# One step of a streaming encoder on one core: three weight blocks begun on 704 tokens, between the adaLN sums

## The chip, the cores and the metric

The kernel runs on one core of one Trainium2 chip. The time is that of the device for one execution, in microseconds (us). Five engines work side by side, each through its own list of instructions in order, and wait for each other by semaphores: TensorE (PE in the profile; PEld is its loading of weights), VectorE (DVE), ScalarE (ACT), GpSimd (POOL) and SyncE (SP), which issues most of the transfers between HBM and SBUF. Results of matmuls land in PSUM, from which ACT or DVE copies them.

## What is computed

One trunk layer on 1024 prompt tokens and 32 sample tokens, each of these two streams with its own conditioning vector c. All arithmetic is in float32. Cut to what the change touches:

```python
mod = silu(c) @ w_ada + b_ada                 # w_ada: 1024 x 6144
sh1, sc1, gt1, sh2, sc2, gt2 = split(mod, 6)
h = rmsnorm(x, g_mix) * (1 + sc1) + sh1       # x: 1056 tokens x 1024 features
u = h @ w_in                                  # 1024 x 5640
qa, ka, va, qm, km, vm, om, ip, fp, ga, gm = split(u)
ya = band_attention(qa, ka, va, rel_bias)     # 8 heads x 64
ym = mlstm(...)                               # 4 heads x 128
merged = sigmoid(ga) * (ya @ w_br_att) + sigmoid(gm) * (ym @ w_br_mlstm)
x = x + gt1 * (merged @ w_out)
# then a second norm, a SwiGLU FFN with its own residual, and a last norm
```

## The kernel before

The activations stand with features on the 128 partitions and the 1056 tokens along the row, in three tiles of 352 tokens (`TILES`). The 1024 features are eight groups of 128, called features 0 to 7 below (`KD` = 8). A matmul in full float32 is made of three in a faster format: every operand is split into a high half (a rounded copy, made by ACT) and a low half (the rest, a subtraction on DVE or POOL), and `PASSES` multiplies high by high, low by high and high by low. So one weight block of 128 output columns costs 8 features x 3 passes = 24 matmuls ("products") of 128x352 for each token tile. `Weights` (W) holds the list of all blocks, loads their raw tiles ahead (three `wraw` buffers) and has them split ahead (four `wsp` half tiles). Buffers of 128 x 2112 floats are taken in turn from one pool of 16 (`slots`), rows of 1056 from a pool of four (`tmp`). The order on PE, ACT, DVE and POOL is the order in which the code is written (`manual_schedule`); SP's transfers are ordered by the framework's scheduler.

The head of the program, with which the change deals, runs so. x is loaded by tokens, eight tiles of 128 tokens and the sample's 32. PE transposes them to features (L281, L295), ACT copies the results to `xTs`, and DVE sums the squares of every token (L273). POOL takes the root of mean square + eps (L298, L299), and `bcast_cols` (L234) lays the 1056 scale factors out as a row over all partitions, `RB`. Meanwhile w_ada's columns for sh1 and sc1 (the first 2048) are loaded as eight tiles `was` of 128 rows, row group by row group. A sum over all 1024 rows is needed for each column, so no column is finished before the last tile is in. The scale sc1 is made on PE (L322): for every tile eight matmuls with the silu of c (`csil`), into one PSUM tile. The shift sh1 is made on DVE (`shift_part`, L309): products of each tile with the silu, accumulated in two rows `acv`, whose sums over partitions PE then takes (`row_sums`, L345).

`first_ada` (L316) and the lines from L1499 on write this order out. Then `first_units` (L467) takes the first two weight blocks, the K and the V block of the first pair of heads, feature by feature: `scaled_x` (L370) multiplies x with the scale and `RB`, `high_h` (L378) adds the shift and rounds, `low_h` (L388) makes the low half, and as soon as one feature of h stands, all 18 products of the two blocks with it run. Their six sums stand in six PSUM banks. After the eighth feature the K and V blocks copy their results (`k_block`, `v_block`), and the Q block (`q_block`) runs as an ordinary block, tile by tile (`unit`, L436). With the next K block begins the attention of the first two heads, whose steps are put between products. Its bias tiles come from a copy of the bias rows in HBM (`rb_d`) by a shifted read, issued when the head begins (`rel_bias_tile`, L688). x by features is also written to HBM (`xres`, L1508) and read again for the residual, much later.

## Time and profile before

| | us |
|---|---|
| median of three runs | 1599.96 (1599.67 to 1600.25) |
| the profiled execution: time | 1597.75 |
| the profiled execution: span, first to last instruction | 1596.1 |
| PE busy | 1566.1 |
| DVE busy | 1126.4 |
| ACT busy | 790.5 |
| POOL busy | 420.0 |

The span is that of the profiled execution, and what lies around it belongs to its time as well. Busy time is counted per engine, and several run at once. A row of a timeline gives the start, the duration, the engine, the line and operation, and the tiles: the one written, an arrow, those read; "x16" merges 16 instructions of a kind, and in square brackets stands how long the engine was idle before and what ended that. A row of a group has, behind the bar, the busy time of all in us and the mean of one in ns. A float32 matmul that is not split by hand shows as two instructions, a transpose as one.

### The profile page before, as it was taken

How to read it: one execution, taken by the hardware profiler on the slowest of the kernel's cores; microseconds unless marked ns; L12 is line 12 of the kernel's file. 1: busy time of each engine (PE TensorE's matmuls, PEld its weight loads, DVE VectorE, ACT ScalarE, POOL GpSimd, SP SyncE). 2: the span in 40 equal slices, each digit the busy share in tenths (PEclk: the TensorE clock that was granted, in tenths of full speed). 3: DMA queues.
4: the chain of work that ended last, by engine and by line, in shares of the span. 5: the costliest groups of instructions: out<-in, count | busy, mean ns of one | idle time of the engine just before them, and what ended most of it. 6: DMA issues, size and time to landing. Idle time of an engine off the chain costs nothing.

```text
span 1596.1 us, 27244 instructions
## 1 busy us (share of the span) xinstructions
PE 1566.1 (98%) x10167; PEld 1546.2 (97%) x10167; DVE 1126.4 (71%) x2291; ACT 790.5 (50%) x1735; POOL 420.0 (26%) x433
## 2 busy tenths in 40 slices
PE   7999999999999999999999999999999999999997
PEld 6989999999999999999999999999999999999997
DVE  7766555556776845546654699899888886799755
ACT  3665463544555545444433655544544444545443
POOL 0343242433222411000012100565565650000000
PEclk9999999999999999999999999999999999999999
DMA  9823323343132332675443311213222227427444
GB/s 364 265 83 94 98 82 109 86 135 110 43 94 67 88 86 75 133 257 176 133 145 112 106 54 54 95 57 103 81 80 94 68 78 252 143 80 249 130 136 155
DMA packets 209569, 193.48 MB, mean 121 GB/s; under 512 B 11530, under 2 KB 179118, under 8 KB 208414
## 3 DMA queue, kind: packets, MB, share of 16 engines
q1 hardware_dynamic: 206894, 189.92, 38.5%
q8 instruction: 80, 1.31, 0.4%
q10 hardware_dynamic: 2512, 1.77, 0.4%
q14 instruction: 51, 0.42, 0.1%
q0 software_dynamic: 32, 0.06, 0.0%
HBM read 153.24 MB, written 41.63 MB: 122 GB/s over the span
## 4 chain that ended last, share of the span: by engine, by line
PE 91%; DVE 3%; ACT 2%; DMA 2%; issue 1%; SPq 0%; POOL 0%; ACTq 0%; DVEq 0%; POOLq 0%
PE mm L443 41%; PE psb L1811 18%; PE mm L1811 11%; PE psb L2193 3%; PE mm L878 3%; PE mm L2193 2%; PE psV L783 2%; PE psb L2057 2%; PE psS L725 2%; PE psT L752 1%; DMA s<-in_w_ada_dram 1%; PE mm L2057 1%; DMA t<-in_x_sample_dram 1%; PE psV L1112 1%; PE mm L475 1%
## 5 line engine op out<-in xcount | busy, mean ns | idle before, releaser
L443 PE MATMUL mm<-s,wsp 128*128 128x352 f32 x4104 | 687.0, 324 | 0.0
L443 PEld LDWEIGHTS mm<-s,wsp 128*128 128x128 f32 x4104 | 657.3, 188 | 1.8 <-issue 0.4
L410 DVE TENSOR_TENSOR wsp<-wraw,wsp 128x512 fp32r<-128x512 f32 (+1 forms) x280 | 235.6, 858 | 114.1 <-ACT wsp L409 103.1
L1811 PE MATMUL psb<-s,wsp 128*128 128x352 f32 x1611 | 271.7, 322 | 1.6 <-DVE wsp L410 0.9
L409 ACT ACTIVATE wsp<-wraw 128x512 fp32r<-128x512 f32 x336 | 199.5, 617 | 142.4 <-PE psb L1811 44.5
L1811 PEld LDWEIGHTS psb<-s,wsp 128*128 128x128 f32 x1611 | 260.5, 188 | 2.1 <-DVE wsp L410 1.1
L1811 PE MATMUL mm<-s,wsp 128*128 128x352 f32 x933 | 159.3, 322 | 0.0
L1811 PEld LDWEIGHTS mm<-s,wsp 128*128 128x128 f32 x933 | 151.2, 188 | 0.5 <-DVE wsp L410 0.5
L745 POOL TENSOR_SCALAR st<-st,mx 128x640 f32<-128x640 f32 (+5 forms) x72 | 53.1, 738 | 186.2 <-DVE mx L744 171.2
L1207 DVE CUSTOM_DVE_ANT_0 junk<-wa,t 128x512 bf16<-128x512 f32 x128 | 94.7, 740 | 3.1 <-DMA wa<-in_w_mod_dram 2.1
L410 POOL TENSOR_TENSOR wsp<-wraw,wsp 128x512 fp32r<-128x512 f32 x56 | 74.9, 1357 | 57.1 <-ACT wsp L409 55.6
L739 DVE CUSTOM_DVE_ANT_0 st<-psS,bias 128x640 f32<-128x640 f32 (+5 forms) x72 | 44.5, 618 | 57.1 <-PE psS L725 41.9
L740 ACT ACTIVATE st<-st,mx 128x640 f32<-128x640 f32 (+5 forms) x72 | 47.9, 666 | 63.4 <-DVE mx L739 62.3
L1758 POOL TENSOR_TENSOR t<-t,sl 128x352 f32<-128x352 f32 x19 | 18.4, 969 | 212.8 <-ACT sl L1756 212.8
L759 ACT ACTIVATE pT<-psT 128x640 fp32r<-128x640 f32 (+3 forms) x80 | 38.7, 493 | 62.6 <-PE psT L752 47.6
L2166 POOL TENSOR_TENSOR fst<-fst,mhalf 128x6 f32<-128x6 f32 x1 | 2.3, 2312 | 221.1 <-DVE fst L2165 221.1
L764 DVE TENSOR_TENSOR pT<-psT,pT 128x640 fp32r<-128x640 f32 (+3 forms) x80 | 44.0, 558 | 22.2 <-ACT pT L759 22.2
L1420 POOL TENSOR_TENSOR wraw<-wraw,raw 128x512 f32<-128x512 f32 x33 | 55.8, 1705 | 0.9
L878 PE MATMUL mm<-s,s 128*128 128x264 f32 (+3 forms) x432 | 54.5, 283 | 0.0
L2193 PE MATMUL psb<-s,wsp 128*128 128x352 f32 x330 | 54.2, 324 | 0.0
L2193 PEld LDWEIGHTS psb<-s,wsp 128*128 128x128 f32 x330 | 53.1, 188 | 0.1
L878 PEld LDWEIGHTS mm<-s,s 128*128 128x128 f32 (+1 forms) x432 | 52.0, 179 | 0.5
(368 smaller groups left out, 2471.6 us busy)
## 6 DMA issues: line engine op xcount, KB each, us to landing
wraw<-in_w_in_dram SPq DMA_DIRECT2D x38, 512.0 KB, 4.0
wraw<-in_w_gate_up_dram SPq DMA_DIRECT2D x33, 512.0 KB, 3.9
wa<-in_w_mod_dram SPq DMA_DIRECT2D x64, 256.0 KB, 2.8
wraw<-in_w_down_dram SPq DMA_DIRECT2D x32, 512.0 KB, 4.3
a_d<-t SPq DMA_DIRECT2D x22, 528.0 KB, 2.7
g_d<-t SPq DMA_DIRECT2D x16, 528.0 KB, 3.2
x<-xres SPq DMA_DIRECT2D x16, 528.0 KB, 7.1
t<-g_d SPq DMA_DIRECT2D x16, 528.0 KB, 4.5
```

Of the source, the lines that this page charges most:

```text
L409: act.activation(dst[:, 0], src, AF.Copy)
L410: eng.tensor_tensor(dst[:, 1], src, f(dst[:, 0]), op=ALU.subtract)
L443: pe.matmul(pt[:, :hi - lo], wt[(w0 + k) // 4][:, a, (w0 + k) % 4], xt[k][:, b, lo:hi], start=(k == 0 and q == 0), stop=(k == n - 1 and q ...
L739: dve.tensor_tensor_reduce(so, sv, bi, -1.0, 3.0e38, ALU.add, ALU.min, mx[:n, 1:2])
L740: act.activation(st[:n, :w], st[:n, :w], AF.Exp, bias=mx[:n, 1:2], scale=-1.0, accum_out=mx[:n, 2:3])
L745: pool.tensor_scalar(st[:n, :w], st[:n, :w], mx[:n, 3:4], 1.0, op0=ALU.mult, op1=ALU.mult)
L878: pe.matmul(pt[:n, :wd], hs[k][:, a, i * P:i * P + n], whl[b][:, k, :wd], start=(k == 0 and q == 0), stop=(k == KD - 1 and q == 2))
L1207: dve.tensor_tensor_reduce(junk, wa, crow[:, c], 1.0, 0.0, ALU.mult, ALU.add, at)
L1420: self.eng.tensor_tensor(a(dst), a(x), a(y), op=op)
L1811: pe.matmul(acc, wt[:, a, k], x[k][:, b], start=(start and not onto and k == 0 and q == 0), stop=(stop and k == 3 and q == 2), skip_group_ ...
L2057: pe.matmul(acc, wt[k // 4][:, u, k % 4], piece_of[k, i][:, v], start=(k == 0 and q == 0), stop=(k == KP - 1 and q == 2))
L2193: pe.matmul(acc, wt[(k - k0) // 4][:, u, (k - k0) % 4], piece_of[k, 2][:, v], start=(k == 0 and q == 0), stop=(k == NF - 1 and q == 2))
```

## The change

The tensors reach the kernel in other layouts. x comes by features (`x_t`: 8 x 128 x 1056, prompt and sample together), so that no transposes are needed. w_in comes by blocks of 128 columns, each partition's 1024 values of a block in one run of 4 KB. The first 2048 columns of w_ada come by feature: tile j has all 1024 rows for the 128 scale columns of feature j, and beside them the 128 shift columns of the same feature, for features 0 to 2 laid out like the scale's, for the others with the columns on partitions and the 1024 rows along the row. So one tile finishes one feature. The bias rows come shifted, 128 x 640 per head. Nothing is written to `xres` or `rb_d`; the residual is read from `x_t`.

The head is written anew:

- The first 704 tokens (two tiles, `CUT`) go ahead, the last 352 follow ("late"). SP loads the early part of x by features, the first adaLN tile in between, then half of the raw weights of three blocks (K, V and Q), the next adaLN tiles, the late part of x, and the rest.
- Squares are taken by ACT over whole feature rows, DVE adds them to one row `acc` (`square_sum`), PE sums that over partitions (`token_sums`), DVE and POOL make the factors (`token_roots`).
- `scale_sums(j)` is eight float32 matmuls for feature j's scale (with `i` = 1, its shift), placed between the products; `scale_done` and `shift_done` finish them on ACT. From feature 3 on the shift comes from `shift_sums`: a multiplication with reduction on DVE, over the row `crow` of the silu of c, once for each stream, finished by ACT.
- For every feature the 18 early products are three blocks x three passes x two tiles. The late tokens follow at the end with two blocks, K and V (48 products); the Q block makes its third tile as an ordinary unit.
- `late_h(k)` makes the late part of the features in three steps, each a feature behind the other: scaling, high half, low half. The sample's 32 columns go through POOL for scaling and low half.
- `put` copies the K block's first tile while the late products run. The loads of the cache and of the first two bias tiles are issued at round 5.

The core of the diff:

```diff
-            sp.dma_start(wa, w_ada[len(was) * P:(len(was) + 1) * P, 0:2048])
+        for i in range(2):
+            sp.dma_start(wa[:, i], w_ada[i, j])
...
+    def scale_sums(j, i=0):
+        at = P * (2 * i + j % 2)
+        for k in range(KD):
+            pe.matmul(psH[:, at:at + P].rearrange("p (r c) -> p r c", c=2), was[j][:, i, k * P:(k + 1) * P],
+                      csil[:, k].unsqueeze(1).to_broadcast([P, DH, 2]), start=(k == 0), stop=(k == KD - 1),
+                      skip_group_check=True)
+    def shift_sums(j, c):
+        dve.tensor_tensor_reduce(junk, was[j][:, 1], crow[:, c], 1.0, 0.0, ALU.mult, ALU.add, sha[:, c, j:j + 1])
+        act.activation(sh1[:, c, j:j + 1], sha[:, c, j:j + 1], AF.Identity, bias=cols[:, R_ADA + j:R_ADA + j + 1])
...
+        for k in range(1, KD):
+            products(k, 0)
+            if k + 2 < KD:
+                scale_sums(k + 2)
+                scale_done(k + 2)
...
+            low_h(k, 0, CUT)
+            if k + 1 < KD:
+                scaled_x(k + 1, 0, CUT)
+                high_h(k + 1, 0, CUT)
...
+            if k + 2 < KD:
+                shift_sums(k + 2, 0)
+            products(k, 1)
...
+            if 1 <= k <= 3:
+                first_high(k - 1, 1)
                 first_low(k - 1, 1)
+            if SHIFT_PE <= k + 1 < KD:
+                shift_sums(k + 1, 1)
+            if k >= 5:
+                late_h(k - 5)
+            products(k, 2)
+            if k == 5:
+                W.loaded = W.split_n = 3
+                W.load(6)
+                early_loads.append(cache_loads())
+                early_loads.extend(rel_bias_tile(h) for h in range(2))
+        for k in range(3, KD + 2):
+            late_h(k)
+            if k == 7:
+                put(*early[0], pts[0][0][:, :NT])
+        put(*early[1], pts[0][1][:, :NT])
+        for k in range(KD):
+            for q in range(3):
+                for i in range(2):
+                    product(k, i, q, 2)
```

Three places of the compiled order. On PE, ahead of the first products and behind them (L322 before and L328 after are the adaLN sums, with a tile `s` of w_ada; L475 the products, with a feature of h and a half tile of a weight): before, the last two of the eight adaLN steps, the row sums and the first products,

```order
L322 MATMUL psT_267<-csil,s_126 128x128 x8
L322 MATMUL psT_267<-csil,s_128 128x128 x8
L348 MATMUL psV_266<-ones,t_268 128x64 x2
L348 MATMUL psV_266<-ones,t_269 128x64 x2
L348 MATMUL psV_266<-ones,t_268 128x64 x2
L348 MATMUL psV_266<-ones,t_269 128x64
L352 MATMUL psV_266<-csil,s_128 128x64
L348 MATMUL psV_266<-ones,t_269 128x64
L352 MATMUL psV_266<-csil,s_128 128x64
L348 MATMUL psT_267<-ones,t_268 128x64
L475 MATMUL mm_426<-s_432,wsp_398 128x352
L475 MATMUL psS_425<-s_432,wsp_400 128x352
```

and now, from the end of the transposes that lay out the token factors:

```order
L227 MATMUL mm_254<-ident,roots 128x64
L475 MATMUL mm_264<-s_268,wsp_246 128x352
L475 MATMUL psS_155<-s_268,wsp_259 128x352
L475 MATMUL psT_153<-s_268,s_262 128x352
L475 MATMUL mm_265<-s_268,wsp_246 128x352
L475 MATMUL psS_155<-s_268,wsp_259 128x352
L475 MATMUL mm_266<-s_268,s_262 128x352
L328 MATMUL psV_154<-csil,s_118 128x128 x16
L475 MATMUL mm_264<-s_268,wsp_246 128x352
L475 MATMUL mm_265<-s_268,wsp_246 128x352
```

Two sums of one feature now stand behind the first six products, where all adaLN sums stood ahead of the first one.

On DVE, one feature's round (L375 and L350: scaling; L392 and L369: low half; L465 and L442: a weight's low half; L337: the shift's reduction and the read of its result). Before, features 2 and 3:

```order
L375 SCALAR_TENSOR_TENSOR s_486<-s_111,s_271,t_265 128x1024
L375 SCALAR_TENSOR_TENSOR s_486<-s_111,s_271,t_265 128x32
L392 SCALAR_TENSOR_TENSOR s_514<-s_486,sh_270,s_514 128x1024
L465 TENSOR_TENSOR wsp_401<-wraw_295,wsp_401 128x512
L375 SCALAR_TENSOR_TENSOR s_545<-s_112,s_271,t_265 128x1024
L375 SCALAR_TENSOR_TENSOR s_545<-s_112,s_271,t_265 128x32
L392 SCALAR_TENSOR_TENSOR s_541<-s_486,sh_270,s_541 128x1024
```

and now a round of one feature, with the beginning of the next:

```order
L369 SCALAR_TENSOR_TENSOR s_368<-s_96,sh_151,s_368 128x704
L350 SCALAR_TENSOR_TENSOR s_96<-s_96,s_152,t_146 128x704
L337 ISA t_147,sha<-s_131,s_102 128x1024
L337 ISA sha 128x1
L442 TENSOR_TENSOR wsp_260<-wraw_100,wsp_260 128x512
L337 ISA t_147,sha<-s_128,s_102 128x1024
L337 ISA sha 128x1
L369 SCALAR_TENSOR_TENSOR s_406<-s_96,sh_151,s_406 128x704
L350 SCALAR_TENSOR_TENSOR s_97<-s_97,s_152,t_146 128x704
```

Two reductions over 1024 elements, with their reads, have come into the round; the rows of 1024 became rows of 704.

On POOL, the sample's columns (L394 before: the low half alone; L352 after: scaling, L371: low half) and the split of a weight (L410). Before:

```order
L394 TENSOR_TENSOR s_541<-s_486,s_541 128x32
L394 TENSOR_TENSOR s_568<-s_545,s_568 128x32
L394 TENSOR_TENSOR s_594<-s_545,s_594 128x32
L394 TENSOR_TENSOR s_621<-s_598,s_621 128x32
L410 TENSOR_TENSOR s_631<-wraw_300,s_631 128x512 x2
L394 TENSOR_TENSOR s_658<-s_598,s_658 128x32
```

and now, all in the late part:

```order
L352 TENSOR_TENSOR s_97<-s_97,t_146 128x32
L371 TENSOR_TENSOR s_368<-s_96,s_368 128x32
L352 TENSOR_TENSOR s_97<-s_97,t_146 128x32
L371 TENSOR_TENSOR s_406<-s_96,s_406 128x32
L352 TENSOR_TENSOR s_98<-s_98,t_146 128x32
L371 TENSOR_TENSOR s_447<-s_97,s_447 128x32
L352 TENSOR_TENSOR s_98<-s_98,t_146 128x32
L371 TENSOR_TENSOR s_484<-s_97,s_484 128x32
L371 TENSOR_TENSOR s_519<-s_98,s_519 128x32
L371 TENSOR_TENSOR s_560<-s_98,s_560 128x32
```

POOL has two operations for each feature, the scaling two features ahead of the low half, where it had one.

More of the change, by code (lines that the diff above doesn't have):

```diff
@@ L334, in first_load @@
[L334 to L353 removed]
+    xTp = [slot([P, 2, T]) for _ in range(KD // 2)]
@@ new lines, in hybrid_stream_step, with in_block, load_ada, load_first @@
+    xTs = [xTp[j // 2][:, j % 2] for j in range(KD)]
+    CUT = TILES[2][0]
+    first_cols = (KA, VA, QA)
+    first_ws = [wraw.tile([P, KD, P], F32, tag="wraw", name=nm("wraw")) for _ in first_cols]
+    was = []
+    def in_block(c):
+        return w_in[(c - GA) // P + 28 if c >= GA else c // P]
+    def load_ada():
+        j = len(was)
+        wa = slot([P, 2, D])
+        for i in range(2):
+            sp.dma_start(wa[:, i], w_ada[i, j])
+        was.append(wa)
+    def load_first(half):
+        for raw, c in zip(first_ws, first_cols):
+            sp.dma_start(raw[:, 4 * half:4 * half + 4], in_block(c)[:, 4 * half:4 * half + 4])
@@ new lines, in silu_cols, with square_sum, token_sums @@
+    def silu_cols():
+        act.activation(csil, cols[:, R_C:R_C + 16].rearrange("p (c k) -> p k c", c=2), AF.Silu)
+        dve.scalar_tensor_tensor(gb1, cols[:, R_ADA + 8:R_ADA + 16], 1.0, gm1, op0=ALU.add, op1=ALU.mult)
+    def square_sum(j, lo, hi):
+        n = hi - lo
+        o = sq2[:, j % 2, :n] if j else acc[:, :n]
+        act.activation(o, xTs[j][:, lo:hi], AF.Square)
+        if j:
+            dve.tensor_tensor(acc[:, :n], acc[:, :n], o, op=ALU.add)
+    def token_sums(a0, n, at, r):
+        for i, a in enumerate(range(0, n, P)):
+            b = min(a + P, n)
+            pe.matmul(tok[:b - a, at + r * i:at + r * (i + 1)], acc[:, a:b], ones[:, 0:1].to_broadcast([P, r]),
+                      start=(i == 0), stop=True, skip_group_check=True)
@@ L473, in product, with products @@
         def product(k, i, q, t):
             (a, b), (lo, hi) = PASSES[q], TILES[t]
-            pe.matmul(pts[i][t][:, :hi - lo], wts[i][k // 4][:, a, k % 4], hs[k][:, b, lo:hi],
+            out = last[i] if t == 2 else pts[i][t]
+            pe.matmul(out[:, :hi - lo], W.blocks[i][3][k // 4][:, a, k % 4], hs[k][:, b, lo:hi],
                       start=(k == 0 and q == 0), stop=(k == KD - 1 and q == 2))
-        for t, (lo, hi) in enumerate(TILES):
+        def products(k, q):
+            for i in range(3):
+                for t in range(2):
+                    product(k, i, q, t)
@@ L521, in first_units @@
+        put(*early[1], pts[0][1][:, :NT])
[3 more added lines that the diff above has]
+                    product(k, i, q, 2)
+        first[id(W.blocks[0])] = {2: last[0][:, :NT]}
+        first[id(W.blocks[1])] = {0: pts[1][0][:, :NT], 1: pts[1][1][:, :NT], 2: last[1][:, :NT]}
+        first[id(W.blocks[2])] = {0: pts[2][0][:, :NT], 1: pts[2][1][:, :NT]}
+        for w, n in zip(W.blocks, (3, 3, 2)):
+            for _ in range(n):
                 W.used(w)
+        W.advance()
@@ L538, in w_cols @@
     def w_cols(c0, home=None):
-        return weight([w_in[:, c0:c0 + P]], KD, 3, home)
+        return weight([in_block(c0)], KD, 3, home)
     plan = []
@@ L1496, in hybrid_stream_step @@
         W.add(w)
-    first_ada()
-    first_split(0)
-    row_sums(0, 0, 2)
-    row_sums(1, 0, 2)
-    row_sums(0, 2, 4)
-    row_sums(1, 2, 4)
-    first_scale()
-    row_sums(0, 4, 5)
-    for j in range(KD):
-        sp.dma_start(xres[j], xTs[j])
-    first_units([run.w for run in segs[0][1][:2]])
+    first_units(segs[0][1][0].put)
     W.ahead = 2
```

401 lines of the change are left out of this document (196 added, 205 removed).

## The prediction

> **What bounds the kernel now.** I read the page first: the shares, the strip of forty slices and the chain of work that ended last.
>
> ```profile
> span 1596.1 us, 27244 instructions
> PE 1566.1 (98%) x10167; PEld 1546.2 (97%) x10167; DVE 1126.4 (71%) x2291; ACT 790.5 (50%) x1735; POOL 420.0 (26%) x433
> ...
> PE   7999999999999999999999999999999999999997
> ...
> PE 91%; DVE 3%; ACT 2%; DMA 2%; issue 1%; SPq 0%; POOL 0%; ACTq 0%; DVEq 0%; POOLq 0%
> ```
>
> TensorE (PE) is busy for 98% of the span and holds 91% of the chain. A change can only gain where PE waits, or by giving it less to do. The strip shows where it waits: the first slice and the last. So the table of stretches comes next (columns: PE, weight loads, DVE, ACT and POOL busy, granted clock, DMA share, GB/s).
>
> ```profile
> 10.00:20.00 10.00, 8.37 (x71) 7.21 (x70) 7.85 (x14) 8.06 (x22) 2.04 (x2) 1.00 1.03 397
> 30.00:40.00 10.00, 8.58 (x72) 8.01 (x72) 8.51 (x11) 1.26 (x2) 0.00 (x0) 1.00 1.06 336
> 40.00:50.00 10.00, 8.81 (x59) 8.25 (x59) 9.87 (x20) 6.59 (x15) 0.62 (x2) 1.00 0.77 281
> 80.00:100.00 20.00, 19.14 (x121) 18.50 (x120) 14.04 (x31) 14.13 (x32) 9.89 (x13) 1.00 0.39 123
> 100.00:120.00 20.00, 17.98 (x127) 17.31 (x127) 10.88 (x26) 13.64 (x24) 6.48 (x8) 1.00 0.15 41
> 200.00:1500.00 1300.00, 1294.96 (x8390) 1284.30 (x8388) 935.26 (x1917) 643.34 (x1419) 354.90 (x340) 1.00 0.36 110
> ```
>
> Up to 40 us PE is partly idle and the DMA engines are full (share 1.03 to 1.06), at 336 to 397 GB/s. From 40 to 50 us DVE is the full one. Stretches of 80 to 120 us hold 2.9 us of idle PE; the 1300 us that follow hold 5.0 in all. The head is the place, so I read PE's timeline there.
>
> ```profile
> 14.63 1.42 PE L281 MATMUL mm<-ident,s 128*128 128x128 f32 x11 [0.96 <-DMA s<-in_x_prompt_dram]
> ...
> 20.69 3.88 PE L322 MATMUL psT<-csil,s 128*128 128x128 f32 x32
> ...
> 35.86 2.05 PE L322 MATMUL psT<-csil,s 128*128 128x128 f32 x16 [0.54 <-DMA s<-in_w_ada_dram]
> ...
> 37.75 1.67 PE L348 MATMUL psV<-ones,t 128*128 128x64 f32 x14
> ...
> 40.97 0.43 PE L475 MATMUL mm<-s,wsp 128*128 128x352 f32 x1 [0.66 <-ACT s L386]
> ```
>
> The last of eight x tiles lands at 14.6, the last adaLN tile at 35.9, and the first product of a block with the features (L475) starts at 40.97. Everything ahead of it is bought by DMA: the products wait until all of x and all of w_ada's first 2048 columns are in.
>
> I need one place where the same work is done in both kernels. It is the end of the 216 products (9 tiles of 24) of the first K, V and Q blocks.
>
> ```profile
> 68.52 5.55 PE L443 MATMUL mm<-s,s 128*128 128x352 f32 x33
> 73.90 0.60 PE L612 MATMUL mm<-ident,t 128*128 128x128 f32 x4
> 74.26 2.17 PE L443 MATMUL mm<-s,s 128*128 128x352 f32 x12
> ...
> 81.25 6.05 PE L443 MATMUL mm<-s,wsp 128*128 128x352 f32 x36
> 87.14 0.34 PE L725 MATMUL psS<-s,s 128*128 128x128 f32 x2
> ```
>
> The Q block ends at 81.25. Two groups of four V transposes stand inside it, 73.90 to 74.26 and one like it, that the changed kernel has later: 0.7 us. So the place stands at **80.5** before. The last two rows give a product: 36 from 81.25 to 87.14, 0.163 each.
>
> **The change part by part.** *The start of the products.* Needed now are the early 704 tokens of x (8 x 0.360 MB) and one adaLN tile (1.05 MB): 3.93 MB, where the last x tile before was the end of 4.19 MB. At 0.397 MB/us (10 to 20 us) this is 0.7 us earlier than 14.63: 13.9. Behind that stands a chain; its prices:
>
> ```profile
> L1756 ACT ACTIVATE sl<-x 128x352 f32<-128x352 f32 x21 | 10.5, 498 | 38.8 <-DVE x L1750 36.5 <-DVE rs L1578 2.2
> L465 DVE TENSOR_TENSOR wsp<-wraw,wsp 128x512 fp32r<-128x512 f32 x4 | 2.6, 680 | 0.0
> L1138 POOL TENSOR_TENSOR dn<-dn,mhalf 128x2 f32<-128x2 f32 x16 | 12.1, 759 | 1.3
> L1588 POOL TENSOR_TENSOR rs<-rs,mhalf 128x4 f32<-128x4 f32 x3 | 3.2, 1081 | 19.5 <-DVE rs L1586 19.5
> L461 ACT ACTIVATE wsp<-wraw 128x512 fp32r<-128x512 f32 x4 | 2.4, 623 | 15.6 <-DMA wraw<-in_w_in_dram 15.6
> L375 DVE SCALAR_TENSOR_TENSOR s<-s,s,t 128x352 f32<-128x352 f32 x4 | 2.2, 578 | 0.1
> L386 ACT ACTIVATE s<-s,sh 128x352 fp32r<-128x352 f32 x4 | 2.2, 588 | 4.3 <-DVE s L375 2.3 <-DVE sh L360 2.1
> ```
>
> Square of 704 on ACT: about 0.8 (0.50 for 352, 0.3 of it growing with size); the addition on DVE 0.9 (0.68 for 512); six sums with ones, seven of them in 1.67 above: 1.4; two small scalings 0.3; the root of three columns on POOL, between 0.76 for two and 1.08 for four: 0.9; three transposes 0.4; copy of the row to SBUF 0.5. That makes 19.1 for the first row. The second root follows on POOL (0.9) and, with some 0.1 for each hand-over between engines, its row is copied at about 20.5. ACT then has two weight copies (0.57 each without overlap) ahead of the first high half, which takes 0.59: **22.2**, 18.8 us ahead of before. Bounds: 21.2 if ACT's copies pack closer, 24.2 if short rows slow the transfers to the 336 GB/s of 30 to 40 us.
>
> *What PE has to do from there to the common place.* 216 x 0.163 = 35.2. The adaLN sums that stood ahead of the products now stand among them: feature 0's two are ahead, features 1 and 2 bring two each, 3 to 7 one each: 9. One is eight matmuls; the row at 20.69 is two such blocks in 3.88, so 1.94: 17.5. Three late token sums and three late transposes: 1.0. In sum 53.7, where before had 35.2 and 11 of the row sums seen at 37.75 (0.24 each, 2.6). Without a wait the place would stand at 75.9.
>
> *Waits among them.* DVE now makes five features' shift rows by a reduction over 1024 elements for each of two streams, and the low halves and scaling for 704 tokens. A round is one feature's 18 early products.
>
> ```profile
> L375 DVE SCALAR_TENSOR_TENSOR s<-s,s,t 128x1024 f32<-128x1024 f32 x6 | 7.6, 1274 | 0.0
> L273 DVE CUSTOM_DVE_ANT_0 t<-s 128x1024 bf16<-128x1024 f32 x8 | 9.7, 1225 | 6.2 <-DMA s<-in_x_prompt_dram 6.0
> L386 ACT ACTIVATE s<-s,sh 128x1024 fp32r<-128x1024 f32 x6 | 6.9, 1153 | 4.4 <-DVE s L375 3.1 <-DVE sh L360 0.7 <-DMA xres<-s 0.6
> ```
>
> 704 lies between 0.578 and 1.274: 0.94, less 0.06 by which such instructions overlap: 0.88. A reduction and its read are 1.24. Rounds 2 and 3 have 2 x 0.88 + 2 x 1.24 + 0.62 for a weight's low half; that low half also waits 0.9 for ACT's copy, which stands on ACT behind the bias that needs the reduction just made. 5.8 on DVE against 18 x 0.163 + 1.94 = 4.9 on PE. Round 1 is even, 4 and 5 are under PE (4.2 and 4.8, the latter with the first late scaling), round 6 is over it by 0.6, as PE has no sum there (2.9). Excess 0.9 + 0.9 + 0.6; a little slack from round 0 goes off it. I take **2.2**; bounds 0.5 (all reductions overlap) and 4.0 (every 704 costs 1.1). ACT has about half of that per round (one high half of 704 at 0.9, a weight copy at 0.6 and small biases) and hides.
>
> *The late third.* 48 products, 0.98 per feature, already in the 216. Beside them DVE has 0.96 (a scaling and a low half of 320 tokens), ACT 1.1, POOL two operations on the sample's 32 columns:
>
> ```profile
> L394 POOL TENSOR_TENSOR s<-s,s 128x32 fp32r<-128x32 f32 x8 | 4.7, 592 | 38.2 <-ACT s L386 36.6 <-DMA xres<-s 1.7
> 64.58 1.24 POOL L394 TENSOR_TENSOR s<-s,s 128x32 fp32r<-128x32 f32 x1
> ```
>
> 2 x 0.59 = 1.18 per feature on POOL, over PE's 0.98; but POOL starts two features ahead, and 0.2 x 8 = 1.6 is covered by that lead. Zero taken, bounds 0 and 6 (the rival below).
>
> So the place stands at 22.2 + 53.7 + 2.2 = **78.1** against 80.5: **-2.4**.
>
> *Behind it.* Before, the Q block was a cushion of 12 us in which ACT and DVE caught up with K and V. Now it is one tile (3.9 us), and all three blocks' copies come at once: about 9 us on ACT (15 copies of 0.46 and three weight copies). The V transposes inside K block 1 wait for a PSUM buffer that ACT frees as the copies end, some 0.4 us. In return the first scores no longer stand behind the cache's low halves on DVE, since those come after them. What PE waited for there:
>
> ```profile
> L553 ACT ACTIVATE s<-mm 64x352 fp32r<-64x352 f32 x20 | 9.1, 456 | 8.8 <-PE mm L443 5.1 <-PE mm L475 3.6
> ...
> 90.30 0.50 PE L725 MATMUL psS<-s,s 128*128 128x256 f32 x2 [0.86 <-DVE mx L739]
> ...
> 103.14 0.63 PE L752 MATMUL psT<-ident,st 128*128 128x128 f32 x4 [0.29 <-DVE pT L764]
> ...
> 106.09 0.59 PE L783 MATMUL psV<-pT,s 128*128 128x256 f32 x3 [1.74 <-ACT pT L759]
> ```
>
> The first wait (0.86) is that queue on DVE; I halve it. The other two come when ACT loads tables for Exp, Silu and Exp again; ACT's rows there keep their order, so they stay. +0.4 - 0.4 = **0**; bounds -2.9 (all three go) and +1.5.
>
> *Nothing on the path:* w_in by block, the shifted bias rows, the copies of x and of the bias that are no longer written to HBM, loads moved in SP's queue. No PE wait of the page names w_in or the bias; full DMA engines hide or free them. If that cover fails, K block 1's raw weights come later: 14.3 MB of first loads and 2.7 MB of bias, cache and raw weights in front of and with them are in at 47 us by 0.4 MB/us, and they are needed at 74.
>
> *The clock.* PE's transposes of 128 x 128 in the first 5 us, and later:
>
> ```profile
> L281 PE MATMUL mm<-ident,s 128*128 128x128 f32 x16 | 3.9, 425 | 5.3 <-DMA s<-in_x_prompt_dram 5.3
> ...
> L281 PE MATMUL mm<-ident,s 128*128 128x128 f32 x49 | 6.5, 284 | 1.6 <-DMA s<-in_x_prompt_dram 1.3 <-ACT s L282 0.3
> ```
>
> 425 ns against 284: PE starts slow. And in the tail, after the last matmul (1586.9):
>
> ```profile
> 1586.62 0.27 PE L2116 MATMUL psb<-ident,x 128*96 128x128 f32 x1
> ...
> 1590.00:1592.00 2.00, 0.00 (x0) 0.00 (x0) 0.40 (x1) 0.76 (x2) 0.00 (x0) 0.50 1.02 378
> ```
>
> the granted clock falls to 0.50. So PE slows when it idles for two or three us, and needs until about 9 us to be fast. In the changed kernel PE has only 2.2 us of work from 14 to 22.2, with a last gap of 2.3 us, so the first products may run slow for some 4 us at a price between 0 and 2.0. I take 0.9. [...]
>
> **Sum:** -2.4 + 0 + 0.9 = -1.5. The profiled execution took 1597.75 us (span 1596.1 and 1.7 around it): 1596.2. The median of the runs is 1599.96, 2.2 above that execution, so **1598.5** there. About 0.2% (3.2 us) is what a measurement of this kernel can tell from no change.
>
> **The rivals.**
> 1. *All waits go.* DVE keeps up (-2.2), the clock stays (-0.9), and attention's waits fall by 1.5. For it: DVE's total from 22 to 66 us (15 operations on 704, 10 reductions, 6 low halves, 7 additions, 4 late ones: 34 us by the prices above) is under PE's 42. Against: its order. 1598.5 - 4.6 = 1593.9.
> 2. *POOL's sample columns become the bound; slower.* Each late feature's third pass waits for POOL's two operations in order. Mean 0.59 us, but the last of them above took 1.24, beside a busy DVE, and DVE is never idle there now. Behind round 7, from about 64.5 us, 13 of them remain, and PE could end the third at 74: from 0.7 us apiece the lead is spent, and at 1.24 they end 6.6 us late: 1605.1. Against: seven of eight before were under 0.9. [...]
> 3. *The early start does not come off.* x by feature has rows of 2816, 1408 and 2048 bytes in place of 4 and 8 KB; at 336 GB/s the start is 24.2 and the gain is spent: 1600.5.
>
> **How the numbers follow.** The forecast has 0.38, rival 3 0.07: no difference, 0.45. Rival 1 and mixtures beyond 3.2 us: 0.33 faster. Rival 2, and DVE's upper bound with the cold clock: 0.22 slower. The range reaches from rival 1 with attention's lower bound (1592.5) to rival 2 (1605). The forecast's own range is 1596 to 1602.
>
> **What would show it.** Right: first L475 product near 22; PE rounds of about 4.9 us with small waits on DVE's low halves and ACT's high halves; the 216 products done near 78; the scores' waits near 103 and 106 still there, some us earlier. Wrong: PE waiting for POOL in the late third; adaLN sums waiting for DMA (each should find its tile landed); matmuls at 0.3 us after 22; attention's first rounds without waits; or a changed stretch after 200 us, where I expect none.

## The result, and the profile after

| us | before | after |
|---|---|---|
| median, 8 runs of each | 1599.62 | 1605.09 (1601.66 to 1606.28) |
| ratio to before, 95% interval | | 1.0031 (1.0020 to 1.0043) |
| the profiled execution: time | 1597.75 | 1605.54 |
| its span | 1596.1 | 1603.5 |
| its mean granted clock | 0.998 | 0.993 |

The changed kernel is slower by about 5 us, where 1598.5 was forecast and 1605.0 was the end of the range. Three executions in the groups of runs of this document (3969 and 5767 us of the kernel before, 3117 us of e13_two) stand far apart, and the ratios leave them out. Of the changed kernel's page, the lines that answer to those shown of before:

```profile
span 1603.5 us, 27214 instructions
PE 1567.5 (98%) x10133; PEld 1547.0 (96%) x10133; DVE 1114.0 (69%) x2296; ACT 798.8 (50%) x1757; POOL 416.2 (26%) x439
...
PE   6989999999999999999999999999999999999997
...
PEclk8999999999999999999999999999999999999999
...
PE 89%; DVE 4%; ACT 4%; issue 1%; DMA 0%; POOL 0%; SPq 0%; ACTq 0%; DVEq 0%; POOLq 0%
```

PE's busy time is the same within 1.4 us and the span is 7.4 longer. The loads no longer stand in the chain (DMA 2% before). What is new is the strip of the granted clock, which starts with an 8. Before it was

```profile
PEclk9999999999999999999999999999999999999999
```

The table of stretches says where (columns as before: PE, weight loads, DVE, ACT, POOL, granted clock, DMA share, GB/s):

```profile
10.00:20.00 10.00, 4.96 (x42) 4.59 (x42) 3.85 (x7) 6.13 (x11) 1.20 (x2) 0.91 1.03 403
20.00:30.00 10.00, 7.96 (x40) 7.12 (x40) 3.84 (x6) 2.92 (x6) 0.49 (x1) 0.58 1.04 409
30.00:40.00 10.00, 9.29 (x76) 9.00 (x75) 6.35 (x10) 5.52 (x14) 0.00 (x0) 1.00 1.03 402
100.00:120.00 20.00, 17.57 (x107) 16.64 (x105) 9.55 (x26) 13.55 (x27) 6.19 (x7) 0.91 0.13 41
```

From 20 to 30 us the clock was at 0.58 (1.00 before), and PE "busy" for 7.96 us did 40 instructions, where it did 76 in 9.29 us right after. From 100 to 120 us it was at 0.91. PE's timeline of the changed kernel, with the places by which the two kernels can be laid beside each other:

```profile
19.72 1.81 PE L227 MATMUL mm<-ident,roots 128*128 128x128 f32 x6 [1.91 <-POOL roots L322]
23.57 0.66 PE L475 MATMUL mm<-s,wsp 128*128 128x352 f32 x1 [2.04 <-ACT s L360]
...
25.50 5.15 PE L328 MATMUL psV<-csil,s 128*128 128x128 f32 x32
...
37.82 2.05 PE L328 MATMUL psV<-csil,s 128*128 128x128 f32 x16 [0.71 <-ACT sh L342]
...
57.72 0.59 PE L475 MATMUL mm<-s,wsp 128*128 128x352 f32 x2 [0.26 <-ACT s L360]
...
66.46 0.59 PE L475 MATMUL mm<-s,wsp 128*128 128x352 f32 x2 [0.60 <-ACT s L360]
...
76.69 0.40 PE L475 MATMUL psT<-s,wsp 128*128 128x352 f32 x1 [0.66 <-POOL s L371]
...
81.90 1.60 PE L417 MATMUL mm<-s,wsp 128*128 128x352 f32 x9
...
95.89 0.62 PE L775 MATMUL psS<-s,s 128*128 128x384 f32 x2 [0.85 <-DVE mx L789]
...
99.82 0.41 PE L802 MATMUL psT<-ident,st 128*128 128x128 f32 x2 [1.38 <-DVE pT L814]
...
107.67 0.63 PE L802 MATMUL psT<-ident,st 128*128 128x128 f32 x4 [0.57 <-DVE pT L814]
...
110.62 0.98 PE L834 MATMUL psV<-pT,s 128*128 128x256 f32 x3 [1.74 <-ACT pT L809]
111.39 4.16 PE L417 MATMUL mm<-s,wsp 128*128 128x352 f32 x18
...
118.92 0.71 PE L802 MATMUL psT<-ident,st 128*128 128x128 f32 x5
```

The same point in the kernel before, from its timeline:

```profile
112.94 0.71 PE L752 MATMUL psT<-ident,st 128*128 128x128 f32 x5
```

The 216 products end at 81.90 against 80.5: 1.4 us late, not 2.4 early. The values' matmuls behind the table loads (two on ACT, 1.28 us each, at 104.20 and 106.95; 99.67 and 102.42 before) start at 110.62 against 106.09: 4.5 late, so attention's first rounds lost another 3.1. The second group of five transposes behind them is at 118.92 against 112.94: 6.0 late, since eighteen products took 4.16 us in place of 3.06. The last 1.4 us of the 7.4 come later: 0.7 until 209 us, 1.5 around 435 (below), and 0.8 of it is won back behind that.

The clock's records in the trace are multiples of 3.413 us long (10.24, 3.41 and 3.41 for the three drops of the changed kernel). Cut at these edges, the stretches around each drop read so (changed kernel):

```profile
14.80:18.22 3.42, 1.56 (x12) 1.38 (x12) 1.21 (x2) 1.88 (x6) 0.00 (x0) 1.00 1.02 404
18.22:21.63 3.41, 1.81 (x6) 0.97 (x6) 0.73 (x4) 1.78 (x5) 1.70 (x2) 0.50 1.03 405
21.63:25.04 3.41, 1.47 (x5) 1.47 (x6) 3.14 (x6) 2.37 (x5) 0.00 (x0) 0.50 1.07 412
25.04:28.46 3.42, 3.42 (x17) 3.42 (x16) 0.25 (x1) 0.00 (x0) 0.00 (x0) 0.50 1.03 413
...
106.96:110.38 3.42, 1.35 (x9) 0.98 (x8) 1.46 (x4) 3.36 (x6) 0.80 (x1) 1.00 0.18 73
110.38:113.79 3.41, 3.17 (x12) 3.20 (x13) 2.21 (x7) 1.09 (x3) 0.65 (x1) 0.50 0.02 5
...
431.23:434.64 3.41, 1.39 (x11) 1.14 (x10) 3.02 (x7) 1.55 (x5) 0.27 (x1) 1.00 0.00 0
434.64:438.06 3.42, 3.42 (x16) 3.07 (x15) 2.16 (x7) 2.99 (x7) 3.42 (x5) 0.50 0.22 81
```

Each time a window in which PE worked for less than half (1.56, 1.35, 1.39 of 3.41 us) is followed by half clock, and it lasts until a window was all but full (3.17 of 3.41 us at 110.38). What such a drop costs can be read near 435. From the end of a 2 us wait of attention (433.81 here, 427.12 before) to the same small matmul (443.92, 435.75) it is 10.11 us with the drop and 8.63 without. The kernel before has the same wait of 1.74 near 106 and one of 1.98 at 427, but its windows' edges cut them, and no drop followed:

```profile
104.67:108.08 3.41, 1.99 (x13) 2.02 (x14) 2.95 (x8) 2.08 (x5) 0.80 (x1) 1.00 0.00 0
425.52:428.94 3.42, 1.82 (x15) 1.71 (x15) 2.55 (x8) 2.53 (x7) 1.25 (x2) 1.00 0.00 0
```

This also orders the runs of the changed kernel: 1601.66 us at a mean clock of 0.996, 1606.28 at 0.992.

### The profile page after: what moved, and what is told of

The parts are those of the page before. It is cut to its first block, busy times and chain, and to the rows that moved or that the text cites. A ratio compares the mean times of both kernels' runs of the same rounds, so it can differ in the third digit from the quotient of the medians.

```text
span 1603.5 us, 27214 instructions
## 1 busy us (share of the span) xinstructions
PE 1567.5 (98%) x10133; PEld 1547.0 (96%) x10133; DVE 1114.0 (69%) x2296; ACT 798.8 (50%) x1757; POOL 416.2 (26%) x439
## 4 chain that ended last, share of the span: by engine, by line
PE 89%; DVE 4%; ACT 4%; issue 1%; DMA 0%; POOL 0%; SPq 0%; ACTq 0%; DVEq 0%; POOLq 0%
PE mm L417 40%; PE psb L1852 18%; PE mm L1852 10%; PE psb L2234 3%; PE mm L929 3%; PE mm L2234 2%; PE psV L834 2%; PE psb L2098 2%; PE psS L775 1%; PE psT L802 1%; PE mm L2098 1%; PE psV L328 1%; PE psV L1163 1%; PE psT L1165 1%; PE psT L1160 1%
## 5 line engine op out<-in xcount | busy, mean ns | idle before, releaser
L789 DVE CUSTOM_DVE_ANT_0 st<-psS,bias 128x640 f32<-128x640 f32 (+5 forms) x72 | 44.5, 618 | 60.2 <-PE psS L775 45.3
```

What stands on the lines that cost most here:

```text
L789: dve.tensor_tensor_reduce(so, sv, bi, -1.0, 3.0e38, ALU.add, ALU.min, mx[:n, 1:2])
```

## The experiments

Two theories came out of this. **A**: the head lost to the half clock. **C**: attention's first rounds lost to the order on DVE, where the work on the cache's keys and values ("the cache's work") stands between two rows of scores. Here is what DVE of the changed kernel does between the first and the third score's row (L789):

```profile
92.91 1.40 DVE L733 TENSOR_TENSOR s<-t,s 64x512 fp32r<-64x512 f32 x2
94.34 0.43 DVE L652 CAST s<-t 128x512 fp32r<-128x512 f32 x1
94.81 0.69 DVE L653 TENSOR_TENSOR s<-t,s 128x512 fp32r<-128x512 f32 x1
95.42 0.42 DVE L789 CUSTOM_DVE_ANT_0 st<-psS,bias 128x256 f32<-128x256 f32 x1
...
97.82 1.06 DVE L604 TENSOR_TENSOR s<-mm,s 64x352 fp32r<-64x352 f32 x2 [1.15 <-ACT kf L602]
98.91 0.56 DVE L789 CUSTOM_DVE_ANT_0 st<-psS,bias 128x384 f32<-128x384 f32 x1
```

The cache's 2.5 us stand ahead of the second score's row. The K tile's low half (L604) waits for ACT's copies, which wait for that row's Exp, and the third row waits for the K tile. All results in one table (ratio to the kernel before, timed in the same group of runs):

| run | median us | ratio, 95% interval |
|---|---|---|
| changed kernel | 1605.09 | 1.0031 (1.0020 to 1.0043) |
| e1_busy | 1611.39 | 1.0078 (1.0065 to 1.0091) |
| e1b_gap1 | 1604.83 | 1.0040 (1.0026 to 1.0054) |
| e5_busy | 1605.92 | 1.0050 (1.0038 to 1.0063) |
| e8_busy | 1603.12 | 1.0026 (1.0016 to 1.0035) |
| e2_cache | 1599.08 | 1.0001 (0.9992 to 1.0010) |
| e3_both | 1605.68 | 1.0046 (1.0033 to 1.0060) |
| e4_busy_cache | 1602.85 | 1.0028 (1.0018 to 1.0038) |
| e9_busy_cache | 1596.98 | 0.9991 (0.9982 to 1.0000) |
| e6_spaced | 1603.59 | 1.0033 (1.0021 to 1.0045) |
| e10_early | 1604.52 | 1.0042 (1.0030 to 1.0055) |
| e11_busy_early | 1602.23 | 1.0022 (1.0012 to 1.0031) |
| e12_late | 1599.96 | 1.0009 (1.0000 to 1.0018) |
| e7_before_cache | 1601.13 | 1.0017 (1.0008 to 1.0026) |
| e16_before_late | 1597.61 | 0.9993 (0.9984 to 1.0002) |
| e13_two | 1605.05 | 1.0039 (1.0025 to 1.0052) |
| e15_layout | 1598.83 | 0.9998 (0.9989 to 1.0007) |
| e14_free | 1596.63 | 0.9986 (0.9977 to 0.9995) |
| e17_all_late | 1598.68 | 1.0000 (0.9991 to 1.0008) |

**PE kept busy ahead of the products.** e1_busy had 20, 12 and 14 calls at the three marked places, e1b_gap1 only the first. The calls add zeros to a region of PSUM into which feature 1's sums are added later, so that the first of those sums no longer clears it (this line of the edit is left out here).

```diff
+    def keep_busy(n):
+        for _ in range(n):
+            pe.matmul(psH[:, P:2 * P], ident, zero, start=not busy, stop=True, skip_group_check=True)
+            busy.append(1)
...
                 scale_sums(0, 1)
+                keep_busy(20)
         token_sums(0, CUT, 0, DH)
+        keep_busy(12)
         scale_done(0)
         shift_done(0)
...
             bcast_cols(RB, roots[:, 1, 3 * i:3 * i + 3], [min(P, hi - a) for a in range(lo, hi, P)], lo)
+        keep_busy(14)
         for i in range(1, 3):
             first_high(i, 0)
```

> The changed kernel with 46 extra matmuls of zeros (128x128, 0.12 us each at full clock) in TensorE's three idle stretches ahead of the first products: 20 after feature 0's adaLN sums (the 3.13 us wait for the token sums), 12 behind the token sums (1.91 us), 14 behind the row's transposes (2.04 us). They add zeros to a region that is summed into later. Theory A (the half clock from 18.2 to 28.5 us is what the head lost): the granted clock stays 1.0 from about 8 us, the first products come every 0.163 us in place of 0.29, the first 32 adaLN matmuls among them take 3.8 in place of 5.15, the 216 products end 2.5 to 3.3 us earlier than at 81.9, and the median falls by about as much, to 1602. Rival B (the chain ahead and VectorE's rounds set the head; the clock only fills their waits): the clock stays high, but waits take the place of the slow matmuls, the products end at 81 to 82 and the median stays within 0.8 us of 1605.1.

Neither. A call is two instructions of 0.116 us, not one, so the extra work overran the gaps, and the first product started at 32.36. The end of the 216 (88.37) came only 6.5 us later for a start 8.8 us later, which speaks for A, but the run doesn't test it.

> Only the first 20 of those extra matmuls, in the longest idle stretch (13.1 to 16.25 us); the two stretches of about 2 us behind it stay idle. Theory A1 (the clock falls when TensorE works in under about half of a window of 3.41 us): the first window is saved, the next one (some 1.3 us of work in 3.41) is not, so the clock falls one window later, near 21.6 us, and most of the price stays: the products end 0 to 1.5 us earlier. Rival A2 (only one idle stretch of about 3 us drops it): with the 3.13 us filled there is no fall at all, and the products end 2.5 to 3.3 us earlier, as with all three stretches filled.

A1, as far as the clock goes: it fell one window later, at 20.9 us, behind a window with 1.45 us of work, and the median hardly moved. So a filled gap of 3 us is not enough; the next window, with two gaps of 2 us, drops it.

e5_busy has 10, 6 and 7 calls.

> The changed kernel with half as many extra matmuls of zeros as in the first try, where each turned out to be two instructions of 0.116 us and the 46 held the chain back by 8.8 us: 10, 6 and 7 calls, 2.3, 1.4 and 1.6 us in the idle stretches of 3.13, 1.91 and 2.04 us. Theory A (the half clock is what the head lost): clock 1.0 from 8 us on, the first product where it was (23.6 to 24.5, the same start of the span apart), products at 0.163 us, the 216 products 2.5 to 3 us earlier from the first product on, median 1602 to 1603. Rival B (VectorE's rounds set the pace once the clock is high): new waits on VectorE or ScalarE of 1.5 us or more among the products, median 1604.3 to 1606.

A miss again, and the timeline says why:

```profile
17.31 1.60 PE L450 MATMUL psV<-zero,ident 128*128 128x128 f32 x12
22.19 1.81 PE L229 MATMUL mm<-ident,roots 128*128 128x128 f32 x6 [3.27 <-POOL roots L324]
```

The second group stood ahead of `scale_done(0)`, which reads the same PSUM tile, so ACT waited for it, and the root came 3 us late. In e8_busy it stands behind `shift_done(0)`:

```diff
         token_sums(0, CUT, 0, DH)
-        keep_busy(12)
         scale_done(0)
         shift_done(0)
+        keep_busy(6)
```

> The changed kernel with the extra matmuls of zeros so placed that they hold nothing back: 10 calls (2.3 us) after feature 0's adaLN sums, 6 (1.4 us) behind the token sums and behind the two reads of those adaLN sums (ahead of these reads they had made ScalarE wait for them, and the chain was 3.3 us late in the second try), 6 behind the row's transposes. Theory A (half clock): no drop of the clock ahead of the products, first product within 0.4 us of where the changed kernel has it against the landing of the parameters, the 216 products 2.5 to 3 us earlier, median 1602 to 1603. Rival B (VectorE's rounds take the place): 1604.3 or more, with waits of 1.5 us or more on VectorE or ScalarE among the products.

```profile
24.23 0.43 PE L487 MATMUL mm<-s,wsp 128*128 128x352 f32 x1 [0.50 <-ACT s L362]
...
25.31 3.73 PE L330 MATMUL psV<-csil,s 128*128 128x128 f32 x32
...
80.31 1.60 PE L419 MATMUL mm<-s,wsp 128*128 128x352 f32 x9
```

Now the clock holds (1.00 in every window from 14.10 to 430.53 us), and the first 32 adaLN matmuls take 3.73 us in place of 5.15. From the first product to the end of the 216 it is 56.1 us in place of 58.3 (81.90 - 23.57): 2.2 less, and no new wait on DVE. The medians agree in all three pairs: 1605.09 to 1603.12, e2_cache to e9_busy_cache 2.1, e10_early to e11_busy_early 2.3. By the ratios to before it is 0.0005, 0.0010 and 0.0020, so 1 to 3 us, and no pair alone is clear of its intervals. The timelines carry the claim: 56.1 us from the first product to the end of the 216 in e8_busy, e9_busy_cache and e14_free alike. Theory A holds, at 2 us rather than 3.

**The cache's work off VectorE.**

```diff
-            dve.tensor_tensor(ck[v, hh], k4[u], f(ck[u, hh]), op=ALU.subtract)
-        split_heads(cv, ckv[:, 1].rearrange("p (h d) -> p h d", d=DH), dve)
+            pool.tensor_tensor(ck[v, hh], k4[u], f(ck[u, hh]), op=ALU.subtract)
+        pool.tensor_scalar(cv[:, :, 0], c3, 1.0, 1.0, op0=ALU.mult, op1=ALU.mult)
+        pool.tensor_tensor(cv[:, :, 1], c3, f(cv[:, :, 0]), op=ALU.subtract)
```

> The changed kernel with the four operations on the cache's keys and values (two low halves of keys, the values' copy and their low half, 2.5 us that VectorE has at 92.9 to 95.4, between the first and the second score's row) given to GpSimd. Theory C (those 2.5 us hold back the second score's row, and each later round starts behind it): the waits of 0.85 and 1.38 us of TensorE near 96 and 99.8 are gone or under 0.4 in sum, the values' matmuls behind the table loads come 2 to 3 us earlier against the end of the 216 products, and the median falls by 2 to 3 us to about 1602.5. Rival D (the lost Q block, TensorE's cushion in which ScalarE and VectorE caught up with K and V): the second score's row comes early, but the K tile's halves and copies hold the following rounds as before; the waits keep 1.5 us or more in sum and the median falls by less than 0.8.

```profile
95.35 0.59 PE L777 MATMUL psS<-s,s 128*128 128x384 f32 x2
95.78 2.09 PE L417 MATMUL mm<-s,wsp 128*128 128x352 f32 x12
98.61 0.44 PE L804 MATMUL psT<-ident,st 128*128 128x128 f32 x2 [0.74 <-POOL st L797]
...
108.55 0.59 PE L836 MATMUL psV<-pT,s 128*128 128x256 f32 x3 [1.73 <-ACT pT L811]
```

The waits of 0.85, 1.38 and 0.57 are gone, one of 0.74 has come. From the end of the products (82.44 here) to the values' matmuls it is 26.1 us in place of 28.7: 2.6 less. The median fell by 6.0 (by the ratios to before 0.0030, 4.8 us). The rest is, as far as the traces show, the clock: without the 0.57 the window around the table loads holds 1.99 us of work, and this execution has no drop near 110 nor near 430 (1.00 in every window from 28.62 us on, up to 1580). At a like mean clock (0.996) the two kernels differ by 3.1 to 3.7 us (1601.66 against 1597.99 to 1598.61).

e3_both and e4_busy_cache join this edit to the first two forms of the extra matmuls and carry their delays.

> Both edits together: the 46 extra matmuls and the cache's four operations on GpSimd. Theories A and C add up: the point where four tiles are transposed for the sixth score is 4.5 to 6 us earlier than in the changed kernel, and the median is about 1599.5 to 1600.5, that of the kernel before. Rivals B and D: within 1.5 us of 1605.1. If only one of A and C holds, about 1602.

> Those extra matmuls, and the cache's four operations on GpSimd (alone 1599.08 us). Theory A: another 2.5 to 3 us off, median 1596 to 1597, 2 us under the kernel before. Rival B: 1598.5 to 1599.5.

Both miss, by what held e1_busy and e5_busy back. e9_busy_cache has the form of e8_busy:

> The same extra matmuls, with the cache's four operations on GpSimd (alone 1599.08 us). Theory A: 1596 to 1597, under the kernel before (1598.4 to 1599.6 in its groups of runs). Rival B: 1598.5 or more.

Theory A, and a version level with or just under the kernel before.

**Is it the place on VectorE?** e6_spaced cuts the work in four pieces, e10_early puts it ahead of the first K tile, e12_late behind the fifth score's row.

```diff
-                side.later.append(lambda: cache_kv(early_loads[0]))
+                for n, part in zip((0, 2, 2, 2), cache_parts(early_loads[0])):
+                    side.later += [lambda: None] * n + [part]
```

> The changed kernel with the cache's work left on VectorE, but in four pieces, each two weight steps (about 2 us) behind the other, in place of 2.5 us at one place. Theory C1 (the place in VectorE's queue ahead of the second score's row is what costs): the waits near 96 and 99.8 fall to under 0.8 in sum, median 1599 to 1600.5, about as with GpSimd. Rival C2 (VectorE has no room for the 2.5 us in these rounds, wherever they stand): each later round is late by its piece, waits of 1.5 us or more in sum, median 1602 or more.

> The changed kernel with the cache's work on VectorE and ScalarE in one piece as it was, but three weight steps earlier: right behind the second group of V's values, ahead of the first K tile's low half, where VectorE stands idle for 2.13 us (87.9 to 90.0). Theory C1 (between the first and the second score's row is the wrong place; the rounds form a chain of VectorE and ScalarE into which nothing fits): the waits near 96 and 99.8 fall from 2.2 to under 0.8 us in sum, the first row is about 0.5 us late, median 1599 to 1601. Rival C2 (any place on VectorE costs the same 2.5 us): median 1603.5 or more.

Both went against C1. In e6_spaced waits of 0.72, 0.90 and 0.57 remain, the first two behind a piece. In e10_early the DVE row and PE's timeline read:

```profile
90.31 1.41 DVE L735 TENSOR_TENSOR s<-t,s 64x512 fp32r<-64x512 f32 x2 [1.83 <-POOL bias L746]
...
94.00 0.29 DVE L791 CUSTOM_DVE_ANT_0 st<-psS,bias 128x128 f32<-128x128 f32 x1
```

```profile
94.36 0.50 PE L777 MATMUL psS<-s,s 128*128 128x256 f32 x2 [1.96 <-DVE mx L791]
```

The idle stretch that I had meant to fill was a wait: the work began only when ACT had made the high halves (89.6 to 90.9, behind the copies of V), whatever releaser the row names. The first row is 2.9 us later than in the changed kernel (2.3 against the end of the products), and PE waits 1.96 at once in place of 0.85 and 1.38. From the end of the 216 to the values' matmuls it is 28.4 us in e10_early and 27.7 in e6_spaced, in place of 28.7. So the 2.5 us cost nearly the same at each place that was tried in this stretch. e12_late takes them out of it, still on VectorE:

```diff
-                for n, part in zip((0, 2, 2, 2), cache_parts(early_loads[0])):
+                for n, part in zip((8, 0, 0, 0), cache_parts(early_loads[0])):
```

> The changed kernel with the cache's work in four pieces on VectorE and ScalarE as in the spaced try, but all of them behind the fifth score's row, where the rounds have 1.3 to 1.8 us of slack on VectorE; its results are needed from the ninth score on. Theory C3 (in the first four rounds ScalarE and VectorE hand each tile back and forth, each round starts when the one before is done, and nothing fits between; later rounds have room): waits near 96 and 99.8 under 0.8 us in sum, median 1599 to 1600, as with GpSimd. Rival C2 (2.5 us more on VectorE cost the same at any place): 1603 or more.

```profile
97.53 0.41 PE L813 MATMUL psT<-ident,st 128*128 128x128 f32 x2
...
105.38 0.63 PE L813 MATMUL psT<-ident,st 128*128 128x128 f32 x4 [0.57 <-DVE pT L825]
```

C3: the waits of 0.85 and 1.38 are gone, and 5.1 us of the median (0.0022 by the ratios, 3.5 us); the stretch to the values' matmuls is 26.1 us, as in e2_cache. The first four rounds are one chain through ACT and DVE; the later ones have room.

e11_busy_early joins e8_busy's matmuls to e10_early:

> The extra matmuls and the cache's work three weight steps earlier, nothing on GpSimd that was not there. Theories A and C1: 1596.5 to 1598.5, under the kernel before. If only C1 holds 1599 to 1601, if only A 1602 to 1603.

Only A shows, as e10_early gave nothing.

**Is it the change that put the work into the chain?**

> The kernel before with the cache's four operations on GpSimd, which asks whether the 6 us that this edit takes off the changed kernel are owed to the change. Theory E (the order of before hid that work: it stood ahead of the first score, beside the Q block's products): only the wait of 0.86 us for the first score's row goes, median 0 to 1 us lower than before. Rival F (the edit helps attention's first rounds as such): 3 us or more lower, 1596 or less.

This try failed to answer: on GpSimd the bias masks came to stand behind the work, and the first row, which needs them, made PE wait 2.38 us in place of 0.86. The kernel before with the late place is the clean form:

> The kernel before with the cache's work in four pieces behind the fifth score's row, the place that took 5.1 us off the changed kernel's median. Theory E (there the Q block's products covered that work, so the change itself made it cost): the wait of 0.86 us for the first score's row goes and nothing else, median 0 to 1 us under the kernel before. Rival F (the move helps attention's first rounds in either kernel): 3 us or more under it.

Theory E: 1.1 us (0.0007 by the ratio), at the edge of what can be told, where the changed kernel gained 0.0022. In e13_two the Q block is an ordinary block again:

```diff
         def products(k, q):
-            for i in range(3):
+            for i in range(2):
                 for t in range(2):
                     product(k, i, q, t)
...
-        first[id(W.blocks[2])] = {0: pts[2][0][:, :NT], 1: pts[2][1][:, :NT]}
-        for w, n in zip(W.blocks, (3, 3, 2)):
+        for w, n in zip(W.blocks, (3, 3)):
```

> The changed kernel with the Q block taken out of the early products: K and V begin on 704 tokens between the adaLN sums, Q's three tiles follow as an ordinary block, as before the change. Theory D (the Q block behind K and V is what let ScalarE and VectorE catch up ahead of attention): the cache's work is done under Q's products, the waits near the second to fourth score are back to 0.9 to 1.2 us in sum (of 2.8, the table loads' 1.74 apart); but a round is now 3.9 us on TensorE against 5.8 on VectorE, so 3 to 5 us of new waits stand among the early products; median 1603 to 1606. Rival D2 (the Q block's place doesn't matter to attention): its waits stay at 2.2 or more in sum, and the median is 1607 or more.

```profile
48.96 0.58 PE L475 MATMUL mm<-s,wsp 128*128 128x352 f32 x2 [0.83 <-DVE s L369]
50.80 0.59 PE L475 MATMUL mm<-s,wsp 128*128 128x352 f32 x2 [0.92 <-ACT s L360]
...
89.27 5.94 PE L417 MATMUL mm<-s,wsp 128*128 128x352 f32 x36
...
97.84 0.50 PE L774 MATMUL psS<-s,s 128*128 128x256 f32 x2 [0.48 <-DVE mx L788]
...
110.68 0.63 PE L801 MATMUL psT<-ident,st 128*128 128x128 f32 x4 [0.29 <-DVE pT L813]
```

Theory D: attention's waits are back to 0.48 and 0.29 (0.86 and 0.29 before the change), and the early products wait for the halves that ACT and DVE make instead. The second K block starts at 89.27 in place of 81.90, and the values' matmuls at 113.63 in place of 110.62. The median is that of the changed kernel all the same: this execution has no drop of the clock near 110 and 435 (1.00 in every window from 26.66 us on, up to 1580). So the place of the Q block trades waits among the products for waits in attention.

e15_layout has two layouts of the change alone, on the kernel before:

```diff
-        return weight([w_in[:, c0:c0 + P]], KD, 3, home)
+        return weight([in_block(c0)], KD, 3, home)
...
-        base = rb_d[h]
-        sp.dma_start(bt, bass.AP(base.tensor, base.offset + 127, [[FLEN - 1, P], [1, WIN]]))
+        sp.dma_start(bt, rel[h])
```

> The kernel before with w_in by block and the bias rows shifted by layout alone (no copy of the bias to HBM, 0.5 MB contiguous per block); x, w_ada and the products as before. Theory N (none of it is on the path): within 0.7 us of the kernel before, the waits of 0.86, 0.29 and 1.74 us in attention's first rounds where they were. Rival L (short rows or the bias's way through HBM cost something): 1.5 us or more lower.

Theory N, within the interval: the blocks of w_in and the shifted bias rows have no part in it that can be told.

**The best version.** e14_free is e9_busy_cache with one more edit (and 4 calls in the second gap):

```diff
-        pts = [psS[:, :512], psS[:, 512:], psA[:, :512], mmt()]
+        pts = [psS[:, :512], psS[:, 512:], mmt(), mmt()]
```

> The best so far (the extra matmuls, the cache's four operations on GpSimd: 1596.98 us) with the broadcast rows of c in a second one of the three small PSUM tiles in place of the half of the tile whose other half takes the token sums: VectorE's reading of these sums stood behind ScalarE's copy of the other half, 0.65 us. Theory: the first product 0.5 to 0.7 us earlier, median 1596.2 to 1596.6. Rival (the weights' copies on ScalarE are next in line): the first product stays, 1596.8 to 1597.2.

The first product starts at 22.18 and the 216 end at 78.26. At 0.9986 (0.9977 to 0.9995) this version is faster than the kernel before by 1 to 4 us.

> The extra matmuls, the freed reading of the token sums (with GpSimd's share of the cache's work 1596.63 us) and the cache's work behind the fifth score's row on VectorE in place of GpSimd: the wait of 0.75 us for GpSimd's scaling near 94 us goes, one of 0.57 for the fifth score's transposed tile comes; median 1596 to 1597.5, faster than the kernel before by 0.1 to 0.2%. If 1598 or more, the late place costs something on VectorE that the waits of the first rounds don't show.

e17_all_late is e14_free with the cache's work behind the fifth score's row on VectorE. A miss: with the late place the wait of 0.57 is back beside the table loads' 1.73, the window there holds 1.36 us of work, and the half clock follows it in this execution (0.50 from 105.72 to 109.14). One profiled execution can't tell how often it does. In these runs the waits predict the time only together with the windows they fall in.

## Why the prediction was wrong

- *The start of the products*, 22.2 (21.2 to 24.2): measured 23.57, in the range. x came as reckoned (403 GB/s, so rival 3's short rows did not slow it). Two things were left out of the chain. DVE's reading of the token sums stood behind ACT's copy of the other half of its PSUM tile, some 0.65 us, and the six transposes ran at half clock: from them to the first product it is 3.85 us, and 3.50 with the clock up. With both removed (e14_free) the first product stands 6.38 us behind the start of the token sums, in place of 7.32. Its 22.18 is not a measure of that by itself, since the whole head lies earlier or later from one execution to the next (24.23 in e8_busy, 22.64 in e9_busy_cache, with the same edit there). About 0.4 of the 1.4 us stays open.
- *PE's work*, 53.7: right. It is 53.7 in e8_busy and e14_free, where the clock is up (1.00 in every window among the products).
- *The waits among it*, 2.2: right in size, but by luck. They were to be DVE's excess in rounds 2, 3 and 6 (0.9, 0.9, 0.6). DVE's low halves of these rounds do stand 6.0 and 5.6 us apart (5.8 was reckoned), but PE has no wait of note in rounds 2 and 3. The four waits that add up to 2.2 are in the timeline above: 0.71 in round 1, where ACT was busy with the late tokens' squares, 0.26 and 0.60 for the high halves of features 5 and 7, and 0.66 in the late third.
- *The clock*, 0.9 (0 to 2.0): the mechanism was right in kind, and the term was mis-sized. I had reckoned with some 4 us of slow products; the half clock held for three windows, 18.2 to 28.5, of which the products had 4.9 us. That cost 2.2 us among them and 0.35 ahead of them. What the term did not contain at all are the later windows that fall under half, 1.5 us near 110 and 1.5 near 435: I took an idle stretch of two or three us as the condition, and in these runs it is how little PE works in a window. None of the 27 windows that dropped the clock (counted in the last section) was wholly idle: 25 of them held 0.36 to 1.56 us of work, the other two 1.91 and 2.10.
- *The late third*, POOL's columns at 0: right. POOL's low half took 0.27 us in the median (0.25 to 0.55) and its scaling 0.50, together under the 0.98 of PE. The one wait of 0.66, named after POOL, is for feature 7's low half: POOL stood idle for 1.72 us ahead of it, since ACT made that feature's high half only behind the copy of K's first tile (73.96 to 74.87). So rival 2 is refuted, and it is chance that its 1605.1 is almost the measured time.
- *Behind it*, 0 (-2.9 to +1.5): **the step that failed**, by 3.1 us. It is the one whose mechanism was wrong. I wrote that the first scores no longer stand behind the cache's low halves, "since those come after them", and stopped there: they come ahead of the second score, and ACT and DVE pass each round on to the next, so they delay all that follow. That the Q block had been "a cushion of 12 us" I had noted, and priced its loss at 0.4. With this step alone put right (e2_cache) the median is 1599.08, near the forecast, though its head still has the slow products: a part of that nearness is luck.
- *Rival 1*, all waits go: refuted. Of the waits at 103 and 106 of before, the first grew from 0.29 to 0.57 and the second stayed at 1.74.
- *Nothing on the path*: right as far as tried (e15_layout, 0.9998); the unwritten copies of x and the moved loads were not tried alone.
- *The sum*: +1.4 at the place, +3.1 behind it, +1.5 near 110 and +1.4 later make the 7.4 of the profiled span. Against the forecast of -1.5 these are 8.9 us: 1.4 at the start, 1.5 of the clock among the products beyond the 0.9, 3.1 behind it, and 2.9 later, where the clock's two drops of 1.5 each are the main part.

What stays open: how much of the 435 us drop belongs to the change. The 2 us wait is in both kernels, and which windows it falls into differs from run to run; e15_layout, at before's time, has that drop too (0.50 from 427.62 to 431.04).

## What to carry over

Work that is moved out of a full engine's way has to be followed to the next place where two engines hand tiles back and forth: here 2.5 us of work cost nearly as much at three positions, and only taking it out of the stretch helped. When a stall is cut into several small waits, count how much the matrix engine works in each 3.4 us; here, with under 1.6 us of work, half clock followed in 25 of 28 cases. Before filling an idle stretch, ask what the waiting instruction waits for: it may be the very work that one wants to put there.
